# One pool per z operand, mid buffers and first weight units of the way down over early operands, and two pairs made side by side

## The chip, the cores and the metric

The kernel runs on one core of one Trainium2 chip. The metric is the device time of one execution in microseconds (us): the median of three runs is 2313.62 us (2311.71 to 2314.23). The profiled execution, from which all times below come, took 2311.51 us; its span from first to last instruction is 2309.7 us, so 1.8 us lie around the span. Its TensorE clock was 0.983 of full speed in the mean.

## The reference, cut to what matters

One layer of a hybrid decoder for 2048 prompt rows and 8 decode rows, model width 1024, feed-forward width 2816, all float32. Two head groups (windowed attention and gated linear attention) give a mixed activation; what follows is:

```python
def finish(x, o_attn, o_gla, r_gla, gla_norm_g, w_o, ffn_norm_g, w_gate, w_up, w_down):
    g = rmsnorm(o_gla, gla_norm_g).reshape(N, T, GLA_WIDTH) * jax.nn.silu(r_gla)
    h = x + jnp.concatenate([o_attn, g], axis=-1) @ w_o
    z = rmsnorm(h, ffn_norm_g)
    return h + (jax.nn.silu(z @ w_gate) * (z @ w_up)) @ w_down
```

The kernel also returns window buffers and recurrent states; the change does not touch what makes them.

## The kernel before, in words

**Precision and products.** Every float32 operand is split into a high part (a ScalarE cast, L92) and a low part (a VectorE subtraction, L93). A product is three matmuls (`mm3`, L104 to L106). Gate, up and down go by a Strassen–Winograd scheme with seven products P1, P6, P2, P7, P5, P4, P3 in this order (`PRODS`); the class `Strassen` reads each product out of PSUM with additions on VectorE (L961) and, for P1, a copy on ScalarE (L1149). Each product thus has its own operand made from sums of quarter blocks, numbered 0 to 6.

**The stages that matter here.**
1. The W_o stage works row tile by row tile: W_o product (`ps_wo`, the 8 decode rows at L1019), the sum h, RMS normalisation to z, transposes on TensorE (`ps_zT`, L1037). For every group of four tiles `operands()` makes the seven operands, splits each into `zhl` (pool of three buffers) and stores it from GpSimd's DMA queue to DRAM as `zc_d` (L1057). h itself is stored by SyncE (SP) to `h_d` and `hdec_d` (L1022).
2. Gate and up. Per half `sb` of the rows, seven operands z0 to z6 (about 2 MB each) are loaded by SP (L1242) and stay in SBUF. For each of 11 pairs of feed-forward blocks, weights are loaded (`wrg`, L1179), their sums are made and split to `whl`, and `prod` runs 12 matmuls a product. In the first half, gate and up take turns product by product on all 512 columns. In the second half the 516 columns (8 decode rows ride along, four in each block) are two pieces of 258, with all seven products of gate ahead of the seven of up. The result silu(gate)*up is called m; its Strassen sums go from GpSimd's DMA queue to `md_d` (L1236). In the second half the decode columns of m are copied to `mdec` on ScalarE (L1227), four copies of 128x4 a pair, 44 in all.
3. The way down. The 11 pairs are four groups (3, 3, 3, 2 pairs). Per group, weights `wrd` (L1270) become seven units `dhl` a pair, in a pool of 22 buffers; then for each of eight row blocks a 1.3 MB mid `mr` is loaded by SP (L1310), split to seven `dm`, and each product sums its three pairs (9 matmuls). Results are added in DRAM by accumulating DMAs (L1329), and the last group writes the output (L1324). The decode rows' products (L1286) use `mhl`, the split `mdec`.

**What sets the order.** The tile framework records the program and a list scheduler with a model of times writes each engine's instruction list; every engine then works strictly in its list's order. Buffers of stages that have ended are reused by address: a new tile waits for the last reader or writer of whatever lay in its bytes. So the place of a pool in SBUF decides what its first loads wait for. In the kernel before, one pool holds z6 to z0; the pool of weight units comes first in the same space and lies with its first unit over the operand of P4 and then over the operands from P1 on; the two `mr` buffers lie at the other end, over the operands of P4 and P3, which are read last.

## Time and profile before

| | before |
|---|---|
| median of three runs | 2313.62 us |
| profiled execution / its span | 2311.51 / 2309.7 us |
| PE (TensorE matmul) busy | 2227.1 us, 96% |
| DVE (VectorE) busy | 1600.5 us, 69% |
| ACT (ScalarE) busy | 957.2 us, 41% |
| POOL (GpSimd) busy | 623.8 us, 27% |
| gate and up | about 959 to 1847 us |
| way down | about 1853 to 2309 us |

A row of the timeline gives the start, the duration, engine, line, operation, output<-inputs, shape and count; in brackets is the engine's idle time before it and what ended it. A row of the windows view gives the stretch, its length, and then for PE, PEld (weight loads), DVE, ACT and POOL the busy us with the count of instructions, then the granted TensorE clock, the share of the DMA engines' time in use, and GB/s. A row of the waits view gives engine, output, line, what it waited for, and the total, the number and the longest of those waits.

### The profile page before, as it was taken

How to read it: one execution, taken by the hardware profiler on the slowest of the kernel's cores; microseconds unless marked ns; L12 is line 12 of the kernel's file. 1: busy time of each engine (PE TensorE's matmuls, PEld its weight loads, DVE VectorE, ACT ScalarE, POOL GpSimd, SP SyncE). 2: the span in 40 equal slices, each digit the busy share in tenths (PEclk: the TensorE clock that was granted, in tenths of full speed). 3: DMA queues.
4: the chain of work that ended last, by engine and by line, in shares of the span. 5: the costliest groups of instructions: out<-in, count | busy, mean ns of one | idle time of the engine just before them, and what ended most of it. 6: DMA issues, size and time to landing. Idle time of an engine off the chain costs nothing.

```text
span 2309.7 us, 34809 instructions
## 1 busy us (share of the span) xinstructions
PE 2227.1 (96%) x12649; PEld 1923.6 (83%) x12649; DVE 1600.5 (69%) x3236; ACT 957.2 (41%) x2120; POOL 623.8 (27%) x791
## 2 busy tenths in 40 slices
PE   8999998999999999699999999999999989999998
PEld 6888886788887788578888889999999968787887
DVE  6787887587776567556666666767676674847477
ACT  5676777343443234323232333333333243535342
POOL 2443434365465133201111110101010122222222
PEclk9999998999998999899999999999999999999999
DMA  7323234245325689872324257323233277878877
GB/s 239 122 75 115 93 108 153 90 157 165 126 87 214 225 275 288 276 247 87 119 79 127 78 177 290 110 84 115 87 111 97 83 225 171 210 165 213 185 184 263
DMA packets 204935, 364.57 MB, mean 158 GB/s; under 512 B 15411, under 2 KB 128332, under 8 KB 200780
## 3 DMA queue, kind: packets, MB, share of 16 engines
q1 hardware_dynamic: 167740, 258.80, 34.2%
q0 software_dynamic: 37024, 103.55, 17.9%
q8 instruction: 100, 1.64, 0.3%
q14 instruction: 71, 0.58, 0.1%
HBM read 211.09 MB, written 152.27 MB: 157 GB/s over the span
## 4 chain that ended last, share of the span: by engine, by line
PE 31%; issue 20%; POOL 5%; DMA 1%; DVE 0%; POOLq 0%; ACT 0%; SPq 0%; DVEq 0%; ACTq 0%
PE ps_b L105 4%; PE ps_b L104 4%; PE ps_b L106 4%; POOL h_d L1329 4%; PE ps_c L105 3%; PE ps_c L104 3%; PE ps_c L106 3%; PE ps_a L105 3%; PE ps_a L106 3%; PE ps_a L104 3%; POOL out_y_prompt_dram L1324 1%; DMA z<-zc_d_P 1%; POOL md_d L1236 1%; DMA zc_d_P<-zhl 0%; DMA wrg<-in_w_gate_dram 0%
## 5 line engine op out<-in xcount | busy, mean ns | idle before, releaser
L104 PE MATMUL ps_b<-z,whl 128*128 128x258 f32 (+1 forms) x792 | 253.8, 321 | 3.2 <-DMA z<-zc_d_P 3.2
L105 PE MATMUL ps_b<-z,whl 128*128 128x258 f32 (+1 forms) x792 | 254.0, 321 | 0.0
L106 PE MATMUL ps_b<-z,whl 128*128 128x258 f32 (+1 forms) x792 | 252.8, 319 | 0.0
L92 ACT CAST dm<-mr 128x384 fp32r<-128x384 f32 (+1 forms) x224 | 108.0, 488 | 188.4 <-PE ps_b L106 97.6
L104 PE MATMUL ps_a<-z,whl 128*128 128x258 f32 (+1 forms) x528 | 170.9, 324 | 8.3 <-DMA z<-zc_d_P 8.3
L105 PE MATMUL ps_a<-z,whl 128*128 128x258 f32 (+1 forms) x528 | 170.7, 323 | 0.0
L106 PE MATMUL ps_a<-z,whl 128*128 128x258 f32 (+1 forms) x528 | 170.3, 323 | 0.0
L104 PE MATMUL ps_c<-z,whl 128*128 128x258 f32 (+1 forms) x528 | 168.6, 319 | 0.9 <-DMA z<-zc_d_P 0.9
L105 PE MATMUL ps_c<-z,whl 128*128 128x258 f32 (+1 forms) x528 | 169.1, 320 | 0.0
L106 PE MATMUL ps_c<-z,whl 128*128 128x258 f32 (+1 forms) x528 | 168.9, 320 | 0.0
L104 PEld LDWEIGHTS ps_b<-z,whl 128*128 128x128 f32 x792 | 149.3, 189 | 15.9 <-DMA z<-zc_d_P 3.5
L106 PEld LDWEIGHTS ps_b<-z,whl 128*128 128x128 f32 x792 | 149.2, 188 | 12.1
L105 PEld LDWEIGHTS ps_b<-z,whl 128*128 128x128 f32 x792 | 149.2, 188 | 11.9
L93 DVE TENSOR_TENSOR dm<-mr,dm 128x384 fp32r<-128x384 f32 (+1 forms) x224 | 114.9, 519 | 59.4 <-ACT dm L92 59.4
L92 ACT CAST whl<-wrg 128x512 fp32r<-128x512 f32 x132 | 81.6, 620 | 150.5 <-PE ps_b L106 81.2
L802 POOL TENSOR_TENSOR bd<-E,qTb 64x128 f32<-64x128 f32 x224 | 127.1, 567 | 60.6 <-ACT E L787 47.2
L93 DVE TENSOR_TENSOR whl<-wrg,whl 128x512 fp32r<-128x512 f32 x132 | 90.9, 688 | 42.9 <-ACT whl L92 42.7
L961 DVE TENSOR_TENSOR gu<-ps_c,gu 128x512 f32<-128x512 f32 (+1 forms) x130 | 77.9, 600 | 61.0 <-PE ps_c L106 60.3
L1236 POOL DMA_DIRECT2D md_d<-m x22 | 15.7, 713 | 373.7 <-DVE m L1199 360.3
L104 PEld LDWEIGHTS ps_a<-z,whl 128*128 128x128 f32 x528 | 100.8, 191 | 17.0 <-issue 4.4
L104 PEld LDWEIGHTS ps_c<-z,whl 128*128 128x128 f32 x528 | 99.8, 189 | 9.3 <-ACT whl L92 1.3
L105 PEld LDWEIGHTS ps_a<-z,whl 128*128 128x128 f32 x528 | 100.5, 190 | 8.2
(385 smaller groups left out, 6625.9 us busy)
## 6 DMA issues: line engine op xcount, KB each, us to landing
mr<-md_d SPq DMA_DIRECT2D x24, 1344.0 KB
zc_d_P<-zhl POOLq DMA_DIRECT2D x49, 512.0 KB, 6.1
wrg<-in_w_gate_dram SPq DMA_DIRECT2D x44, 512.0 KB
wrg<-in_w_up_dram SPq DMA_DIRECT2D x44, 512.0 KB
nT_d<-nT SPq DMA_DIRECT2D x16, 1024.0 KB
zT<-nT_d SPq DMA_DIRECT2D x8, 2048.0 KB
z<-zc_d_P SPq DMA_DIRECT2D x7, 2064.0 KB
z<-zc_d_P SPq DMA_DIRECT2D x7, 2048.0 KB
```

The lines of the kernel that those rows point to most:

```text
L92: nc.scalar.copy(h, src)
L93: (eng or nc.vector).tensor_tensor(l, src, h.bitcast(F32), ALU.subtract)
L104: nc.tensor.matmul(ps, lh, rh, start=start, stop=False, skip_group_check=more)
L105: nc.tensor.matmul(ps, lh, rl, start=False, stop=False, skip_group_check=more)
L106: nc.tensor.matmul(ps, ll, rh, start=False, stop=stop, skip_group_check=more)
L802: nc.gpsimd.tensor_tensor(bv[rows, :, h], eo, qo, ALU.mult)
L961: nc.vector.tensor_tensor(out, a, b, ALU.add)
L1236: nc.gpsimd.dma_start(md_d[sb][g][:, :, q, fp - GROUPS[g][0], :], src.rearrange("p (m t) -> p m t", m=4))
L1324: nc.gpsimd.dma_start(O["y_prompt"][0, ti * P:(ti + 1) * P, cols], hq[which])
L1329: nc.gpsimd.dma_start(h_d[ti][:, cols], c, accum_op=ALU.add)
```

## The change

1. Each z operand gets a pool of its own, and the pools stand in the order of the products. The addresses of z0 to z6 come out the same.
2. The 44 copies to `mdec` go from ScalarE to GpSimd.
3. On the way down the `mr` pool is placed first, so its two buffers lie over z0 and z1 (read by P1 and P6). The weight units come in three pools of 7, 7 and 8, used in turn; the first unit lies over z2 and z3, the others of the first pair over z1 and z2, the next two pairs over z3 to z6.
4. In the first group the units of pairs 1 and 2 are made side by side, one product of each at a time.

```diff
@@ gate and up
-        zcp = pool(ph, "g_zc", 1, side="right")
+        zcp = {name: pool(ph, f"g_z{q}", 1, side="right") for q, name in enumerate(PRODS)}
...
-                    nc.scalar.copy(mdec[:, 2 * fp + f, 4 * j:4 * j + 4], m[:, 512:516])
+                    nc.gpsimd.tensor_copy(mdec[:, 2 * fp + f, 4 * j:4 * j + 4], m[:, 512:516])
...
-            zc = {name: zcp.tile([P, 2, 4, 516], F32R, tag=f"z{q}", name=f"z{q}")[:, :, :, :WIDTHS[sb]]
-                  for q, name in reversed(list(enumerate(PRODS)))}
+            zc = {name: zcp[name].tile([P, 2, 4, 516], F32R, tag=f"z{q}", name=f"z{q}")[:, :, :, :WIDTHS[sb]]
+                  for q, name in enumerate(PRODS)}
@@ way down
-        wdp = pool(ph, "d_w", 22, side="right")
         mrp = pool(ph, "d_mr", 2, side="right")
+        wdps = [pool(ph, f"d_w{i}", n, side="right") for i, n in enumerate((7, 7, 8))]
+        made = [0]
+
+        def unit_tile():
+            j = made[0] % 22
+            made[0] += 1
+            return wdps[min(j // 7, 2)].tile([P, 2, 512], F32R, tag="w", name="dhl")
...
-            us = []
-            for p in range(p0, p1):
+            us = [{} for p in range(p0, p1)]
+
+            def pair_units(p):
...
-                    hl = wdp.tile([P, 2, 512], F32R, tag="w", name="dhl")
+                    hl = unit_tile()
                     split(hl[:, 0], hl[:, 1], src)
-                    uq[q] = hl
-                us.append(uq)
+                    us[p - p0][q] = hl
+                    yield
+
+            for some in ([[p0], [p0 + 1, p0 + 2]] if g == 0 else [[p] for p in range(p0, p1)]):
+                for _ in zip(*[pair_units(p) for p in some]):
+                    pass
```

The instruction lists differ in two places: where gate and up begin, and where the way down begins (with small moves behind it on the way down). Between them TensorE's list is the same. Line numbers of the changed kernel are 1 higher from L1165 on and 10 to 13 higher on the way down.

**SP where gate and up begin.** `h_d_4838` is the store of the last row tile's h, `hdec_d` that of the decode rows; the numbers 4840 to 4846 at `zc_d_P` are the operands of P1, P6, P2, P7, P5, P4, P3. Before:

```order
L1179 DMA wrg<-in_w_gate_dram 128x4x256
L1022 DMA h_d_4838<-h 128x1024
L1022 DMA hdec_d<-h 8x1024
L1242 DMA z_10184<-zc_d_P_4840 128x8x512
L1242 DMA z_10183<-zc_d_P_4841 128x8x512
L1242 DMA z_10182<-zc_d_P_4842 128x8x512
L1242 DMA z_10181<-zc_d_P_4843 128x8x512
L1242 DMA z_10180<-zc_d_P_4844 128x8x512
L1242 DMA z_10179<-zc_d_P_4845 128x8x512
L1242 DMA z_10178<-zc_d_P_4846 128x8x512
```

And now, in the same place of SP's list:

```order
L1180 DMA wrg<-in_w_gate_dram 128x4x256
L1243 DMA z_10196<-zc_d_P_4840 128x8x512
L1022 DMA h_d_4838<-h 128x1024
L1243 DMA z_10197<-zc_d_P_4841 128x8x512
L1243 DMA z_10198<-zc_d_P_4842 128x8x512
L1243 DMA z_10199<-zc_d_P_4843 128x8x512
L1022 DMA hdec_d<-h 8x1024
L1180 DMA wrg<-in_w_gate_dram 128x4x256
L1180 DMA wrg<-in_w_up_dram 128x4x256
L1243 DMA z_10202<-zc_d_P_4846 128x8x512
L1243 DMA z_10200<-zc_d_P_4844 128x8x512
L1243 DMA z_10201<-zc_d_P_4845 128x8x512
```

The load for P1 moved ahead of the last row tile's store, those for P6, P2 and P7 ahead of the decode rows' store; two weight loads and the load for P3 now stand ahead of those for P5 and P4.

**ACT in the same place.** `zhl` are the casts of the second half's last group of row tiles, `b_9842` to `b_9845` the transposed quarter blocks, `t_10118` to `t_10121` their sums; `gp` is the copy of gate's first product and `whl` are casts of weights. Before:

```order
L1030 ACTIVATE z,ss<-h 8x1024
L92 CAST zhl<-b_9842 128x528
L92 CAST zhl<-t_10119 128x528
L92 CAST zhl<-b_9843 128x528
L92 CAST zhl<-t_10120 128x528
L92 CAST zhl<-t_10118 128x528
L92 CAST zhl<-t_10121 128x528
L92 CAST zhl<-b_9845 128x528
L1149 COPY gp_10193<-ps_a 128x512
```

And now:

```order
L1030 ACTIVATE z,ss<-h 8x1024
L92 CAST whl<-sx 128x512 x2
L92 CAST zhl<-b_9842 128x528
L92 CAST zhl<-t_10119 128x528
L92 CAST zhl<-b_9843 128x528
L92 CAST whl<-sx 128x512
L92 CAST whl<-wrg 128x512
L92 CAST zhl<-t_10120 128x528
L92 CAST zhl<-t_10118 128x528
L92 CAST zhl<-t_10121 128x528
L92 CAST zhl<-b_9845 128x528
L1149 COPY gp_10211<-ps_a 128x512
```

Four casts of weights, whose buffers the products P1 and P6 of gate and up must first release, now stand between and ahead of the `zhl` casts. On TensorE, all 24 matmuls of P1 (and no longer only those of the W_o stage) stand ahead of the decode rows' transposes of z.

**DVE where the way down begins.** `uu`, `gu` and `up` are partial results of up and the products with gate, `dm` the split mids, `dhl` the split weight units, `ty` and `tx` sums of weights. Before, from behind the last product of up on:

```order
L93 TENSOR_TENSOR dhl<-wrd,dhl 128x512
L961 TENSOR_TENSOR up_17944<-gu_17942,gu_17943 128x512
L958 TENSOR_TENSOR uu_17946<-m_17940,gu_17942 128x512
L93 TENSOR_TENSOR dhl<-ty,dhl 128x512
L93 TENSOR_TENSOR dhl<-wrd,dhl 128x512
L958 TENSOR_TENSOR uu_17945<-up_17944,m_17940 128x512
L93 TENSOR_TENSOR dhl<-tx,dhl 128x512
L93 TENSOR_TENSOR mhl<-mdec,mhl 128x22x8
L958 TENSOR_TENSOR ty<-wrd,ty 128x512
L958 TENSOR_TENSOR gu_17942<-gp_17941,uu_17945 128x512
L958 TENSOR_TENSOR tx<-wrd 128x512
L93 TENSOR_TENSOR dm<-mr,dm 128x384 x7
```

And now, from the fourth product of up (P7) on:

```order
L961 TENSOR_TENSOR uu_17964<-ps_b,up_17962 128x258 x2
L93 TENSOR_TENSOR dm<-mr,dm 128x384 x3
L961 TENSOR_TENSOR uu_17964<-ps_c,uu_17964 128x258
L93 TENSOR_TENSOR dhl<-wrd,dhl 128x512
L93 TENSOR_TENSOR dhl<-ty,dhl 128x512
L1200 TENSOR_TENSOR gu_17961<-uu_17964,gu_17961 128x258
L93 TENSOR_TENSOR dhl<-wrd,dhl 128x512
L961 TENSOR_TENSOR uu_17964<-ps_c,uu_17964 128x258
L93 TENSOR_TENSOR dhl<-tx,dhl 128x512
L958 TENSOR_TENSOR ty<-wrd,ty 128x512
L93 TENSOR_TENSOR dm<-mr,dm 128x384
L961 TENSOR_TENSOR up_17962<-ps_b,up_17962 128x258
```

The splits of mids and of the first units moved from behind the last result of up to between the results of its products P7 to P3.

More of the change, by code (lines that the diff above doesn't have):

```diff
@@ L1272, in group @@
                 r0, r1 = raws
-                uq = {}
-                b = (r0[:, 0:512], r0[:, 512:], r1[:, 0:512], r1[:, 512:])
-                for q, src in zip(PRODS, sums_b(*b)):
-                    hl = wdp.tile([P, 2, 512], F32R, tag="w", name="dhl")
+                for q, src in zip(PRODS, sums_b(r0[:, 0:512], r0[:, 512:], r1[:, 0:512], r1[:, 512:])):
+                    hl = unit_tile()
                     split(hl[:, 0], hl[:, 1], src)
-                    uq[q] = hl
-                us.append(uq)
+                    us[p - p0][q] = hl
[3 more added lines that the diff above has]
+                    pass
             def decode():
```

## The prediction

> **What bounds the kernel now.** I read the page first, for the busy shares, then the view of TensorE's waits, then windows over the two places where the instruction lists differ, and then each engine's timeline there.
>
> ```profile
> PE 2227.1 (96%) x12649; PEld 1923.6 (83%) x12649; DVE 1600.5 (69%) x3236; ACT 957.2 (41%) x2120; POOL 623.8 (27%) x791
> ...
> PE ps_a L104 <- DMA z<-zc_d_P: 8.3, 2, 4.3
> ...
> PE ps_zT L1037 <- DVE z L1032: 6.9, 1, 6.9
> PE ps_a L104 <- ACT dm L92: 6.5, 1, 6.5
> ...
> PE ps_b L104 <- DMA z<-zc_d_P: 3.2, 2, 3.0
> ...
> PE ps_c L104 <- ACT dhl L92: 2.2, 1, 2.2
> ...
> PE ps_c L104 <- DMA z<-zc_d_P: 0.9, 1, 0.9
> ```
>
> TensorE is busy 96% of the span, and the change neither adds a matmul nor removes one. Only its idle time and its slow clock can give anything. Four of its waits belong to the start of gate and up (8.3 + 6.9 + 3.2 + 0.9 = 19.3 us, three of them for a z operand), and 6.5 + 2.2 us to the start of the way down.
>
> ```profile
> 940.00:1010.00 70.00, 50.62 (x198) 37.73 (x196) 28.28 (x47) 18.61 (x31) 11.11 (x14) 0.85 0.99 335
> 1820.00:1875.00 55.00, 45.28 (x285) 37.43 (x284) 38.67 (x73) 22.61 (x50) 6.43 (x9) 0.91 0.45 166
> 1875.00:2309.00 434.00, 427.05 (x1879) 346.74 (x1877) 287.11 (x512) 163.90 (x332) 105.30 (x136) 1.00 0.80 198
> ```
>
> In the first window the DMA engines are full (0.99); in the second they are not (0.45). Behind 1875 TensorE is busy 427 of 434 us, so the small moves there can neither win nor lose much; I cost them at 0. That is the cover: if it were gone, the 7 us of idle time in that row would be at stake.
>
> **Part 1, the z operands (about 938 to 1012 us).**
>
> ```profile
> 938.39 7.67 PE L1019 MATMUL ps_wo<-WO,mixdec 128*40 128x512 f32 x32
> ...
> 959.10 0.80 PE L104 MATMUL ps_a<-z,whl 128*128 128x512 f32 x1 [4.28 <-DMA z<-zc_d_P]
> ...
> 970.62 0.51 PE L104 MATMUL ps_b<-z,whl 128*128 128x512 f32 x1 [3.02 <-DMA z<-zc_d_P]
> ...
> 982.03 0.76 PE L104 MATMUL ps_a<-z,whl 128*128 128x512 f32 x1 [4.03 <-DMA z<-zc_d_P]
> ...
> 996.34 0.47 PE L104 MATMUL ps_c<-z,whl 128*128 128x512 f32 x1 [0.93 <-DMA z<-zc_d_P]
> ...
> 938.52 0.33 SPq L1022 DMA_DIRECT2D h_d<-h  x1
> 950.34 0.29 SPq L1022 DMA_DIRECT2D hdec_d<-h  x1
> 950.81 40.70 SPq L1242 DMA_DIRECT2D z<-zc_d_P  x7
> ```
>
> P1 begins at 959.10, P6 at 970.62, P2 at 982.03, P5 at 996.34; each needs about 5.5 us of TensorE (24 matmuls at 0.23 us), so 959 to 982 holds 11 us of work. The first load leaves SP only behind the decode rows' store, at 950.81, and P1 starts 8.3 us later. In the changed list that load stands ahead of the last tile's store (938.52) and waits only for the W_o matmuls whose weights lie in its bytes, so it can leave near 938 and land by 950.
>
> P1 then waits for something else, a PSUM bank that VectorE frees with the first low-part addition of the decode rows:
>
> ```profile
> 947.61 0.68 DVE L582 TENSOR_TENSOR h<-ps_wo,h 8x512 f32<-8x512 f32 x1
> ...
> 954.69 0.63 ACT L92 CAST zhl<-b 128x528 fp32r<-128x528 f32 x1 [3.20 <-issue]
> ...
> 964.68 0.63 ACT L92 CAST zhl<-t 128x528 fp32r<-128x528 f32 x1 [6.61 <-DMA zc_d_P<-zhl]
> ...
> 974.71 0.63 ACT L92 CAST zhl<-b 128x528 fp32r<-128x528 f32 x1 [3.45 <-DMA zc_d_P<-zhl]
> 975.25 0.58 ACT L1149 COPY gp<-ps_a 128x512 f32<-128x512 f32 x1
> ```
>
> That is 948.3, so P1 runs from about 949 to 955, ten us earlier than before, and P6 when z1 lands (issued behind the decode matmuls at 946, so by about 957). This gain does not reach the end of the stage. P2 reuses the bank that ScalarE's copy of P1 frees, and this copy stands in ScalarE's list behind the last `zhl` cast (974.71 here), which waits for a `zhl` buffer and so for an earlier store to `zc_d` to land. Before, that was hidden, since z2 came at 982.03. In the changed order it becomes the gate, and it slips: two weight casts that wait for P1, and two that wait for P6, now stand among the `zhl` casts, and on TensorE the decode rows' transposes, from which all of these casts come, stand behind P1. By hand, P1's end at 955 to 956.5 against the first `zhl` cast's 954.69 shifts the chain by 1.5 to 3.5 us, the copy ends at 977.3 to 979.3, and P2 starts near 978: **4 us** earlier than 982.03. P5, at 996.34 before, follows two products later at about 992. Its load waits for its own store, the third from the end, and by my replay lands by 990, so it doesn't decide. On SP it now stands behind the load for P3 and behind two weight loads, which wait for buffers that VectorE frees once P6 is done, near 964; neither is due before 990 either. Bounds: if P2 starts no earlier than before, 0; if the chain doesn't slip (P2 at 975.9) and TensorE stays at full clock, 6 us, and 8 if the 0.93 us before P5 and the slow stretch behind P2's pause go as well.
>
> The clock is part of that price.
>
> ```profile
> 960.00:965.00 5.00, 5.00 (x13) 3.84 (x13) 0.00 (x0) 0.32 (x1) 0.71 (x1) 0.51 1.03 373
> ...
> 980.00:985.00 5.00, 2.97 (x7) 2.42 (x8) 0.80 (x2) 0.00 (x0) 0.00 (x0) 0.70 1.06 327
> ```
>
> Behind P1's pause 13 matmuls took 5 us at clock 0.51 where 0.23 us each makes 3.0; behind P2's, 7 took 2.97 us where 1.6 would do. A pause of about 4 us is thus followed by a slow stretch that costs 1.3 to 2 us and more. In the changed kernel P2 follows one pause of some 14 us; I charge it the stretch that it had before (1.3); were it twice as long, 1.3 us of the 4 would go, which the bounds hold. By the Trainium skill, "TensorE: Matmul & The Clock Gate" (Part 1, the HAM clock gate), the clock drops to half after an idle window of about 3.4 us and comes back after as long a busy one, whatever the length of the pause; by that one long pause costs no more than a short one, about 1.7 us, and the sum would change by less than half a us. The row of 960 to 965 agrees in kind, though at half clock for all of its 5 us.
>
> **Part 2, the copies to mdec.**
>
> ```profile
> 1836.01 0.19 ACT L1227 COPY mdec<-m 128x4 f32<-128x4 f32 x1 [5.84 <-DVE m L1199]
> ...
> L802 POOL TENSOR_TENSOR bd<-E,qTb 64x128 f32<-64x128 f32 x224 | 127.1, 567 | 60.6 <-ACT E L787 47.2
> ...
> L1236 POOL DMA_DIRECT2D md_d<-m x22 | 15.7, 713 | 373.7 <-DVE m L1199 360.3
> ```
>
> 44 copies of 0.19 us are 8.4 us off ScalarE, which is 41% busy: no gain in themselves. On GpSimd the trace has no such copy; the nearest row is a 64x128 operation of 0.57 us, 32 times as wide, so each costs something between nothing and 0.6 us. It sits idle for 360 us before the `md_d` stores, so 0 either way. What the move does is clear ScalarE's list: the copy shown waited 5.84 us for a result, and everything behind it with it. Through that they belong to part 3.
>
> **Part 3, the start of the way down.**
>
> ```profile
> 1847.05 0.80 SPq L1310 DMA_DIRECT2D mr<-md_d  x2
> ...
> 1852.95 2.99 ACT L92 CAST dm<-mr 128x384 fp32r<-128x384 f32 x7 [4.36 <-DMA mr<-md_d]
> ...
> 1853.52 0.80 PE L104 MATMUL ps_a<-dhl,dm 128*128 128x512 f32 x1 [6.50 <-ACT dm L92]
> ...
> 1847.06 0.43 DVE L961 TENSOR_TENSOR uu<-ps_c,uu 128x258 f32<-128x258 f32 x1 [0.55 <-PE ps_c L106]
> ...
> 1854.13 3.36 DVE L93 TENSOR_TENSOR dm<-mr,dm 128x384 fp32r<-128x384 f32 x7
> ```
>
> Before, the first `mr` leaves at 1847.05, when the last z operand is read, and lands 5.9 us later (1852.95); TensorE stands from 1847.0 to 1853.52.
>
> ```profile
> 1835.00:1840.00 5.00, 5.00 (x44) 5.00 (x43) 1.42 (x4) 0.19 (x1) 0.71 (x1) 1.00 0.18 52
> ...
> 1850.00:1855.00 5.00, 1.48 (x4) 0.90 (x5) 5.00 (x10) 2.05 (x5) 2.32 (x4) 0.50 0.99 390
> 1855.00:1860.00 5.00, 5.00 (x14) 3.07 (x13) 5.00 (x11) 4.59 (x10) 0.00 (x0) 0.58 1.03 401
> 1860.00:1865.00 5.00, 2.77 (x12) 1.41 (x10) 4.32 (x8) 2.05 (x4) 0.00 (x0) 1.00 0.99 382
> ...
> 1870.00:1875.00 5.00, 4.68 (x19) 2.81 (x19) 4.94 (x9) 2.74 (x6) 0.59 (x1) 1.00 0.00 0
> ```
>
> From 1850 to 1860 VectorE is full, and up to 1875 TensorE runs 12 to 19 matmuls in 5 us where it could run 22: the stage is bound by the splits. About 67 matmuls are done from 1847 to 1875; at 0.23 us they are 15.4 of 28 us, so 12.6 us are lost.
>
> In the changed kernel the `mr` buffers lie over z0 and z1, free when up's P6 has been read. Up's products take 2.9 us each (24 matmuls at 0.12 us) and the last ends at 1847.0, so P6, five products ahead, ends at about 1833; the load lands 5.9 us later, at 1839, with the DMA engines at 0.18. Seven `dm` splits (3.36 us on VectorE) and four units (4 x 0.6 us) then run before 1847, in a VectorE that is busy 1.42 of 5 us: 5.8 us of the work that bound the stage moves ahead. The first product can start once VectorE has read the last of P3 (1847.06 before, about 1.5 us later with the splits between), near 1849 against 1853.52. Replaying the list from there I count 57 matmuls by 1865 and a full TensorE behind, against 67 by 1875; 57 x 0.23 is 13.1 of 18, so 4.9 us are lost in place of 12.6. That is 7.7 us; I take **7**, as the second part of VectorE's list is rough. Bounds: 3 us, if only the earlier start of 4.5 counts and the units of pairs 1 and 2 give some back, and 10, if all waits and the slow clock go and only the start at 1849 is left. Side-by-side units are in this count: each product needs the units of three pairs.
>
> **The sum.** 4 + 7 = 11 us, from the profiled 2311.51 to 2300.5. The median of the runs lies 2.1 us above the profiled run, which would make it 2302.6. I say **2302 us**.
>
> **The rivals.** (a) The forecast, 2302, with 2298 to 2306 as its own range.
>
> (b) Only the way down gains. P2 starts at 982 as before, because the `zhl` stores, which share full DMA engines with loads that now start 13 us earlier, land later. For it: the DMA engines are at 0.99 in that window. Against: before 955 the trace has room. Time: 2313.6 - 7 = 2306.6.
>
> (c) Both gain at their bound: 8 + 10 = 18, so 2295.6. Against it, the chain of `zhl` casts can hardly fail to slip.
>
> (d) The change doesn't do what it says: the way down stays bound by VectorE (3 us gained) and the z operands give 0: 2310.6. VectorE's row of 1870 to 1875, still 4.94 of 5 us busy, speaks for it.
>
> (e) Slower, by one mechanism: the slow `zc_d` store.
>
> ```profile
> zc_d_P<-zhl POOLq DMA_DIRECT2D x7, 528.0 KB, 9.4
> zc_d_P<-zhl POOLq DMA_DIRECT2D x6, 512.0 KB, 5.2
> ```
>
> Stores to `zc_d` land in 5.2 us in the median without z loads beside them and in 9.4 us with them. Two landings in a row stand between the third and the last `zhl` cast, and the last cast gates P2. From 978 each further us of landing delays P2 by two: at 2 us more the first part gains nothing, and only from about 8 us more (17 us each) is P2 12 us later than before, which outweighs the 7: 2313.6 - 7 + 12 = 2318.6. By the Trainium skill, "DMA: Bandwidth & Descriptors" (Queues, rings and completion order), an engine takes turns between the queues that have work, packet by packet. By that a store beside one queue of loads gets half the rate however many loads stand behind, so its landing should stay near 9.4 us, which speaks against (e); the two rows above agree, no run yet shows it with earlier loads.
>
> **How the numbers follow.** (a) 0.57, (b) 0.20, (c) 0.08, (d) 0.09, (e) 0.06. About 0.2%, 4.6 us, is what a measurement of this kernel can tell from no change. Faster by more than that: (a), (b) but for its upper edge, and (c), 0.83. Within it: (d) and that edge, 0.13. Slower: most of (e), 0.04. Case (a) and most of (b) and (c) make the range 2295 to 2309.
>
> **What would show it.** In the changed profile: the first z load near 938 and P1 near 949; TensorE's longest wait there before P2, near 978, ended by ScalarE's `gp` copy and not by a z load; P5 at about 992. On the way down: `mr` issued near 1833 less the 4 us of the first part, the `dm` casts about 6 us behind, the first matmul within 2.5 us of the last of up, no slow clock there, and TensorE full from 18 us behind the last of up. Wrong would be: a TensorE pause before up's P3 (mids that land more than 3 us late would hold VectorE ahead of the additions that free its banks), `zc_d` landings above 12 us, or a window on the way down behind 1875 with less than the 427 of 434 us.

## The result, and the profile after

The changed kernel is slower: a median of 2319.06 us (ten runs, 2314.7 to 2322.57) against 2312.1 us for the kernel before in the same rounds (ten runs, 2309.08 to 2316.36). The ratio is 1.0029 with a 95% interval of 1.0019 to 1.0038, so some 7 us were lost where 11 were forecast as gained. The profiled execution has a span of 2317.4 us, 7.7 us more than before.

The page of the changed kernel (first row) and its view of TensorE's waits:

```profile
PE 2221.5 (96%) x12649; PEld 1916.7 (83%) x12649; DVE 1595.7 (69%) x3236; ACT 951.2 (41%) x2076; POOL 642.7 (28%) x835
...
PE ps_a L104 <- ACT gp L1149: 23.1, 2, 22.9
...
PE ps_b L104 <- DMA z<-zc_d_P: 1.7, 1, 1.7
...
PE ps_a L104 <- DMA z<-zc_d_P: 1.1, 1, 1.1
```

TensorE's busy time is about what it was (2227.1 us before). The waits for a z operand (8.3 + 3.2 + 0.9 us over five places before) have shrunk to 1.7 + 1.1 us, and the 6.5 us for `dm` are gone. In their place stands one wait of 22.9 us for ScalarE's copy `gp`, the largest of the whole program. The windows view shows in which stretch the time went; the kernel before first, then the changed one:

```profile
935.00:1010.00 75.00, 55.62 (x224) 41.49 (x223) 31.71 (x53) 18.69 (x31) 13.67 (x17) 0.86 0.96 323
```

```profile
935.00:1010.00 75.00, 44.29 (x181) 32.64 (x181) 30.45 (x50) 18.68 (x31) 12.65 (x16) 0.77 0.98 320
...
1875.00:2318.00 443.00, 431.51 (x1889) 347.89 (x1887) 290.47 (x519) 166.01 (x337) 105.88 (x136) 1.00 0.78 195
```

Where gate and up begin, 181 matmuls were done in 75 us where 224 had been; at 0.23 us each the 43 missing ones are 9.9 us. Behind 1875 TensorE is now idle for 443 − 431.5 = 11.5 us instead of 7.

To compare runs I use stretches between events, since the part up to the W_o stage, whose instruction lists are the same in all kernels here, scatters by −4.2 to +3.6 us from one profiled execution to another. The first stretch goes from the last W_o matmul of a row tile to the last matmul of up: 909.64 us before (937.38 to 1847.02), 919.48 us after (935.05 to 1854.53), **+9.8 us**. From there on I follow ScalarE's copy `c<-ps_a`, of which there is one a row block, eight a group. The rows of the eighth, sixteenth and twenty-fourth, before and after:

```profile
1973.62 0.59 ACT L1327 COPY c<-ps_a 128x512 f32<-128x512 f32 x1
...
2094.39 0.59 ACT L1327 COPY c<-ps_a 128x512 f32<-128x512 f32 x1
...
2214.64 0.59 ACT L1327 COPY c<-ps_a 128x512 f32<-128x512 f32 x1
```

```profile
1976.63 0.59 ACT L1340 COPY c<-ps_a 128x512 f32<-128x512 f32 x1
...
2097.40 0.59 ACT L1340 COPY c<-ps_a 128x512 f32<-128x512 f32 x1
...
2219.72 0.59 ACT L1340 COPY c<-ps_a 128x512 f32<-128x512 f32 x1 [0.59 <-PE ps_a L106]
```

From the end of up to the eighth copy it is 126.60 us before and 122.10 after: **−4.5 us**, the gain at the start of the way down. The next group costs the same in both, the third 122.32 against 120.25 us (**+2.1**), and the stretch to the last store of the output another **+2.6 us**. Together +10.0 us, of which the early scatter of this profile (937.38 to 935.05, −2.3) leaves the 7.7 us between the spans.

**Where the 22.9 us come from.** First TensorE at the start of gate and up, in the changed kernel's timeline, then SP's issues there:

```profile
935.05 0.39 PE L106 MATMUL ps_wo<-WO,mt 128*128 128x512 f32 x1
...
951.81 0.77 PE L104 MATMUL ps_a<-z,whl 128*128 128x512 f32 x1 [1.08 <-DMA z<-zc_d_P]
...
991.05 0.80 PE L104 MATMUL ps_a<-z,whl 128*128 128x512 f32 x1 [22.89 <-ACT gp L1149]
```

```profile
935.47 0.59 SPq L1243 DMA_DIRECT2D z<-zc_d_P  x1
...
943.77 14.81 SPq L1243 DMA_DIRECT2D z<-zc_d_P  x3
958.68 4.64 SPq L1022 DMA_DIRECT2D hdec_d<-h  x1
963.42 0.76 SPq L1180 DMA_DIRECT2D wrg<-in_w_gate_dram  x1
...
978.66 19.63 SPq L1243 DMA_DIRECT2D z<-zc_d_P  x3
```

The loads do leave early (935.47 against 950.81), and P1 starts at 951.81 against 959.10. P2 waits for the bank that `gp` reads. ScalarE and VectorE, the changed kernel:

```profile
960.69 0.63 ACT L92 CAST zhl<-b 128x528 fp32r<-128x528 f32 x1
...
989.88 0.63 ACT L92 CAST zhl<-b 128x528 fp32r<-128x528 f32 x1 [11.54 <-DMA zc_d_P<-zhl]
990.42 0.58 ACT L1149 COPY gp<-ps_a 128x512 f32<-128x512 f32 x1
...
980.62 0.69 DVE L958 TENSOR_TENSOR sy<-wrg,sx 128x512 f32<-128x512 f32 x1 [11.08 <-DMA wrg<-in_w_gate_dram]
...
982.23 2.59 POOL L1057 DMA_DIRECT2D zc_d_P<-zhl  x3 [14.74 <-DVE zhl L93]
```

Read backwards: `gp` stands behind the last `zhl` cast; that cast waits until an earlier `zhl` buffer has been stored; the store waits for VectorE's `zhl` subtractions; and VectorE had been idle for 11.08 us, because a sum of the *second* pair's weights stands ahead of three of them in its list and the load of those weights, issued at 963.42 behind the three z loads and the `hdec_d` store, landed only at 980.6, 17 us later. On top of that the chain starts late: the first `zhl` cast is at 960.69 instead of 954.69.

### The profile page after: what moved, and what is told of

Its sections match the earlier page's. It is cut to its first block, busy times and chain, and to the rows that moved or that the text cites. A ratio compares the mean times of both kernels' runs of the same rounds, so it can differ in the third digit from the quotient of the medians.

```text
span 2317.4 us, 34789 instructions
## 1 busy us (share of the span) xinstructions
PE 2221.5 (96%) x12649; PEld 1916.7 (83%) x12649; DVE 1595.7 (69%) x3236; ACT 951.2 (41%) x2076; POOL 642.7 (28%) x835
## 4 chain that ended last, share of the span: by engine, by line
PE 77%; issue 6%; DVE 6%; DMA 5%; POOL 3%; ACT 2%; SPq 0%; POOLq 0%; DVEq 0%; ACTq 0%
PE ps_b L105 7%; PE ps_b L104 7%; PE ps_b L106 7%; PE ps_a L105 5%; PE ps_a L104 5%; PE ps_a L106 5%; PE ps_c L105 5%; PE ps_c L104 5%; PE ps_c L106 5%; PE ps_d L104 3%; PE ps_d L106 3%; PE ps_d L105 3%; PE ps_wo L104 2%; PE ps_wo L106 2%; PE ps_wo L105 2%
## 5 line engine op out<-in xcount | busy, mean ns | idle before, releaser
L104 PE MATMUL ps_a<-z,whl 128*128 128x258 f32 (+1 forms) x528 | 170.7, 323 | 24.0 <-ACT gp L1149 22.9
L104 PEld LDWEIGHTS ps_a<-z,whl 128*128 128x128 f32 x528 | 100.8, 191 | 33.1 <-ACT gp L1149 23.3
L92 ACT CAST whl<-sy 128x512 fp32r<-128x512 f32 x88 | 54.7, 621 | 152.3 <-PE ps_b L106 88.7
L105 PEld LDWEIGHTS ps_a<-z,whl 128*128 128x128 f32 x528 | 100.4, 190 | 8.2
L106 PEld LDWEIGHTS ps_a<-z,whl 128*128 128x128 f32 x528 | 100.3, 190 | 7.8
```

Of the source, the lines that this page charges most:

```text
L92: nc.scalar.copy(h, src)
L104: nc.tensor.matmul(ps, lh, rh, start=start, stop=False, skip_group_check=more)
L105: nc.tensor.matmul(ps, lh, rl, start=False, stop=False, skip_group_check=more)
L106: nc.tensor.matmul(ps, ll, rh, start=False, stop=stop, skip_group_check=more)
```

## The experiments

Each kernel was timed in five rounds beside the kernel before; ratios are to it, with their 95% interval. `issue_after(x)` in the diffs puts an instruction behind x in the list of the same engine and adds nothing else. One table of stretches for all of them, each as the difference to the kernel before, from the profiled executions:

| kernel | W_o to end of up | to end of group 1 | group 2 | group 3 | to the end | ratio |
|---|---|---|---|---|---|---|
| the change | +9.8 | −4.5 | 0.0 | +2.1 | +2.6 | 1.0029 |
| e1 | +8.2 | −2.6 | 0.0 | 0.0 | +0.1 | 1.0026 |
| e2 | −0.4 | −3.6 | +0.8 | +2.4 | +1.5 | 0.9997 |
| e3 | +4.7 | −6.0 | −0.6 | +1.9 | +2.0 | 1.0015 |
| e4 | +0.6 | −2.5 | +3.8 | +2.0 | +2.7 | 1.0019 |
| e5 | +0.3 | −3.6 | +2.9 | +2.1 | +0.9 | 0.9997 |
| e6 | −0.6 | −3.3 | +0.9 | +3.6 | +1.0 | 1.0007 |
| e7 | +7.0 | −6.0 | −0.4 | +1.8 | +1.5 | 1.0007 |
| e8 | −0.2 | −3.6 | +1.6 | 0.0 | 0.0 | 0.9993 |
| e9 | +0.1 | 0.0 | −0.1 | 0.0 | 0.0 | 1.0001 |
| e11 | +8.0 | −4.3 | −0.7 | 0.0 | 0.0 | 1.0012 |
| e12 | +7.3 | −3.6 | −0.7 | 0.0 | +1.2 | 1.0017 |
| e13 | −0.4 | −3.2 | +0.2 | +0.5 | 0.0 | 0.9975 |
| e14 | −2.5 | −3.7 | −0.7 | +0.6 | +0.1 | 0.9964 |
| e15 | −3.9 | −8.2 | +0.5 | +2.0 | +1.3 | 0.9970 |

The sum of a row lies within 1.5 us of the difference of the medians for ten of the fifteen, and 1.9 to 3.3 us off for the change, e5, e7, e13 and e14; so single entries under about 2 us are not read as effects. e2 and e5 show why: they differ only in the engine of the `mdec` copies and have the same ratio, and yet stand 2.1 us apart in group 2.

### e1: the z pools alone

```diff
 kernel before, with
-        zcp = pool(ph, "g_zc", 1, side="right")
+        zcp = {name: pool(ph, f"g_z{q}", 1, side="right") for q, name in enumerate(PRODS)}
```

> The kernel before with the first part of the change alone (a pool for each z operand); the copies to mdec, the mr pool, the unit pools and the order of the units stay as before. Where gate and up begin, the instruction lists of SP, ACT, DVE and PE come out as in the changed kernel. Theory: the loss is made at this place. The load of the second pair's weights stands on SP behind three z loads; VectorE's list has the sum of these weights ahead of three low parts of zhl; so the stores to zc_d, the last zhl cast, the gp copy and P2 are late. Then P2 starts near 991 as in the changed kernel (982.0 before), and the time is 7 to 9 us above the kernel before, about 2320. Rival: the loss is made on the way down, and this kernel is within 2 us of the kernel before or faster by up to 4.

Measured: 2316.57 against 2310.72 us, ratio 1.0026 (1.0016 to 1.0036). TensorE in its timeline:

```profile
989.59 0.79 PE L104 MATMUL ps_a<-z,whl 128*128 128x512 f32 x1 [22.07 <-ACT gp L1149]
```

The same picture as in the changed kernel, with 8.2 of its 9.8 us; VectorE stands 10.10 us for the second pair's weights. One part of the change, the z pools, carries the loss, some 6 us here where 7 to 9 were expected.

### e2: everything but the z pools

```diff
 the change, with
-        zcp = {name: pool(ph, f"g_z{q}", 1, side="right") for q, name in enumerate(PRODS)}
+        zcp = pool(ph, "g_zc", 1, side="right")
```

> The changed kernel without its first part: one pool for the seven z operands as before, but the copies to mdec on GpSimd, the mr buffers over z0 and z1, unit pools and units of pairs 1 and 2 side by side. Theory: the start of the way down gains about 4 us (the lag of the changed kernel falls from 7.5 us at the last products of up to 3.5 us at the end of the first group), and up to 4 us of it are lost again where later groups begin; so 0 to 4 us below the kernel before. Rival, the prediction's count for this part: 7 us below. Rival on the other side: this part is what makes the changed kernel slow, 3 us or more above the kernel before.

Measured: 2309.91 against 2310.72 us, 0.9997 (0.9989 to 1.0006), no difference. The start of gate and up is as before (−0.4 us). The start of the way down gains 3.6 us, and groups 2 to 4 give 4.7 back (0.8 + 2.4 + 1.5). One thing limits this run as a trial of the rest. The mids do load 14.4 us ahead of the end of up, but the splits of mids and units stand behind it in VectorE's list: VectorE is busy for 5.10 of the last ten us of up, as in the kernel before, and for 8.99 in the change. e4, e5, e6, e8 and e9 share this order, so none of them has the list that the prediction replayed. Two questions were left: what at the start of gate and up makes the early loads harmful, and what the later groups lose on.

### e3: the second pair's weight work behind the last zhl subtraction on VectorE

```diff
 the change, with
+                if (sb, fp) == (0, 1):
+                    with tc.issue_after(last_zhl_subtraction):
+                        pair(sb, fp, zc)
```

> The changed kernel with one edge more: VectorE's work on the second pair of gate and up stands behind the last low part of zhl in VectorE's list, so that no zhl waits for the load of these weights. SP's and ACT's lists stay. Theory (VectorE held by the weight sum): the idle time of 11.1 us ahead of three zhl parts goes, P2 starts near 979 to 982 in place of 991, and the time falls by 8 to 10 us against the changed kernel, to about 2310. Rival (the stores to zc_d land late because the z loads fill the DMA engines, as the prediction's slower case has it): the stores take as long to land, P2 starts within 2 us of 991 and the time stays at 2317 to 2319.

Measured: 2313.5 against 2310.72 us, 1.0015 (1.0005 to 1.0025). In its timeline P2 still waits, but less:

```profile
986.53 0.80 PE L104 MATMUL ps_a<-z,whl 128*128 128x512 f32 x1 [16.38 <-ACT gp L1150]
```

Counted from the last W_o matmul (937.89 here) P2 comes at 48.6 us, against 56.0 in the changed kernel and 44.7 before. The sum that waits for the late weight load is thus worth 7.4 of the 11.4 us at P2 and 5.1 us of the stretch (9.8 to 4.7), where 8 to 10 us had been expected. It is the largest single piece, but not all; and since the stores still land beside early loads here, slower stores aren't the main cause.

### e7: all of that weight work behind the last zhl, on ScalarE too

```diff
 e3, and
+                if 7 <= made_u[0] < 28:   # units 8 to 28: the rest of the first pair's, the second's
+                    behind the last zhl cast (ScalarE) and subtraction (VectorE)
```

> The whole change, with all weight work of the first pair from its eighth unit on and of the second pair behind the last zhl on both ScalarE and VectorE, so that the zhl chain waits for neither P1, P6 nor a weight load; on SP one weight load in place of two stands ahead of the last z loads. Theory: the chain starts some 6 us earlier than in the run where only VectorE's work was moved, P2 starts near 979, the stretch from the last W_o tile to the last product of up takes 908 to 911 us (919.5 in the changed kernel, 914.3 with only VectorE's work moved, 909.6 before), and the time is 2 us above to 3 us below the kernel before. Rival (the DMA engines bound this stage, so the loads land no earlier and P2 only moves to about 984): 2 to 4 us above.

Measured: 2315.34 against 2313.36 us, 1.0007 (0.9997 to 1.0017).

```profile
981.92 0.80 PE L104 MATMUL ps_a<-z,whl 128*128 128x512 f32 x1 [13.04 <-ACT gp L1157]
...
977.20 0.52 SPq L1251 DMA_DIRECT2D z<-zc_d_P  x1
982.23 0.39 SPq L1188 DMA_DIRECT2D wrg<-in_w_gate_dram  x1
988.06 5.22 SPq L1251 DMA_DIRECT2D z<-zc_d_P  x2
```

P2 is at 44.9 us behind the last W_o matmul, as early as before; the slipped casts were another 3.7 us. Yet the stretch still costs +7.0 us, more than in e3, where 2 us less to 1 us more than before had been expected. The reason is the second piece of the same mistake: P5, two products on, waits 5.1 us for its operand, whose load stands on SP behind the load for P3 and a weight load. It leaves 51.1 us behind the last W_o matmul, against 42.5 in the kernel before.

### e11: the decode rows' transposes ahead of P1, and one unit pool

```diff
 e7, with one pool of 22 units on the way down as before, and
+                if (sb, fp) == (0, 0):
+                    with tc.issue_after(last_transpose):
+                        pair(sb, fp, zc)
```

> The whole change with one pool for the units, the zhl chain ahead of later weight work on ScalarE and VectorE, and on TensorE the decode rows' transposes ahead of P1, so that the chain of zhl waits for nothing that comes from the early loads. z loads stay early. Theory A (the early loads are worth what room the DMA engines had, 2.8 us by their shares between 940 and 955, and only what stood ahead of the zhl chain spoiled it): P2 starts near 978, the stretch from the last W_o tile to the last product of up takes 906 to 909 us (909.6 before), the way down gains 6 us and keeps them; 6 to 9 us below the kernel before. Theory B (earlier loads slow the stores to zc_d and h_d and give nothing): the stretch takes 910 us or more; 4 to 6 us below.

Measured: 2313.8 against 2311.13 us, 1.0012 (1.0003 to 1.002).

```profile
978.40 0.79 PE L104 MATMUL ps_a<-z,whl 128*128 128x512 f32 x1 [7.71 <-ACT gp L1158]
...
1001.52 0.76 PE L104 MATMUL ps_c<-z,whl 128*128 128x512 f32 x1 [9.57 <-DMA z<-zc_d_P]
```

The `zhl` chain is repaired: P2 comes at 41.3 us, 3.3 us earlier than before, which is what the prediction had expected of it (978). All of it is lost again at P5, which waits 9.57 us, and the stretch still stands at +8.0. Two gates lie side by side at this place; opening this one alone does not bring the stretch back. No run opens the other one alone.

### e12: the z loads behind the decode rows' store

```diff
 e11, and
+                if sb == 0:
+                    with tc.issue_after(hdec_d_store):
+                        the seven z loads
```

> The run with the transposes first, with the one difference that all seven z loads stand behind the store of the decode rows' h on SP, as in the kernel before. Theory A: the stretch from the last W_o tile to the last product of up takes 909 to 911 us as before, 2 to 3 us more than with the early loads; the way down gains 6 us; 5 to 6 us below the kernel before. Theory B: no slower than with the early loads.

Measured: 2314.6 against 2311.13 us, 1.0017 (1.0008 to 1.0026). The early loads are gone and the loss is not (+7.3 us, where theory A had none); P5 waits again:

```profile
998.69 0.77 PE L104 MATMUL ps_c<-z,whl 128*128 128x512 f32 x1 [6.48 <-DMA z<-zc_d_P]
```

So what is left of the loss does not need loads that leave early, nor the DMA time that these take from others; the candidate that remains is the order of the last three z loads among themselves and against the weight loads.

### e13: z loads in the products' order, the second pair's weights behind them, all behind the store

```diff
 e12, and
+                each z load behind the one of the product before; the second pair's wrg loads behind the last
```

> The run with the z loads behind the decode rows' store, with one difference: on SP the seven z loads go in the order of the products and the second pair's weight loads stand behind all of them, as in the kernel before (there the load for P3 and a weight load stood ahead of those for P5 and P4, and P5 waited 6.5 us for its operand). Theory: the stretch from the last W_o tile to the last product of up is 909 to 911 us as in the kernel before (917.0 with the load for P3 ahead); the way down gains 3 to 5 us and keeps them, since it has one pool of units; 3 to 5 us below the kernel before. Rival: the stretch stays above 912 us, and the place of the load for P3 was not its cause.

Measured: 2308.37 against 2314.32 us, 0.9975 (0.9966 to 0.9985). Nothing waits for P5's operand any more, and the stretch is back at −0.4 us. The edit from e12 to e13 touches SP's order alone: it is worth 7.7 us. The load for P5 now leaves 42.1 us behind the last W_o matmul, where it left at 48.0 in e12. The edit moves the load for P3 and the weight loads at once, so the two are not told apart.

### e14: the same with the early loads

```diff
 e13 without "behind the store": the first four z loads leave as early as in the change
```

> As the run with the z loads in turn, but the first four of them early as the change has them: ahead of the last tile's and the decode rows' stores. The one difference between the two is when the loads can leave. Theory A (early loads win the room that the DMA engines had): the stretch is 906 to 908.5 us, 2 to 3 us less than with the late loads, and the time 5 to 8 us below the kernel before. Theory B (the stage is bound by the DMA engines and the chain of stores, early loads win nothing): within 1 us of the run with late loads.

Measured: 2304.86 against 2314.32 us, 0.9964 (0.9951 to 0.9977). Its timeline:

```profile
978.72 0.80 PE L104 MATMUL ps_a<-z,whl 128*128 128x512 f32 x1 [8.78 <-ACT gp L1158]
...
944.96 14.15 SPq L1256 DMA_DIRECT2D z<-zc_d_P  x3
...
979.38 9.19 SPq L1256 DMA_DIRECT2D z<-zc_d_P  x3
988.63 8.00 SPq L1189 DMA_DIRECT2D wrg<-in_w_gate_dram  x2
```

SP is held for 14.15 us by three loads just as in the changed kernel, but what stands behind them is no longer needed soon. P2 is at 978.7, and the stretch gains 2.5 us. With the late loads of e13 it was −0.4, so the early loads win some 2 us, about as much as single entries can show; the medians of the same rounds, 2304.86 and 2308.37, go the same way, though their intervals overlap.

### e4, e5, e6: the parts of the way down, and the loads of later groups

```diff
 e4: e2, with every pair's units made one pair after the other
 e5: e2, with nc.scalar.copy(mdec...) as before
 e6: e2, and in groups 2 and 3
+                if g in (1, 2) and mi == 1: the second mid's load behind the fifth weight load of the group
```

> The kernel before with the copies to mdec on GpSimd, the mr buffers over z0 and z1 and the unit pools, but the pairs' units one after the other; z operands in one pool as before. Against the run without the z pools (which had the pairs side by side and was 0.8 us below the kernel before, with 4 us gained at the start of the way down and given back where the third and fourth groups begin). Theory: side by side costs. Pair 2's weights cannot be loaded until pair 0 has given back two of the four raw buffers (VectorE stood 3.9 us for that load), and SP's list of the third group puts two mids ahead of weight loads; without it SP's list of the third group is again as in the kernel before. So 3 to 6 us below the kernel before. Rival: side by side is what gives the 4 us, and without it the time is within 1 us of the kernel before.

> The kernel before with the mr buffers over z0 and z1, the unit pools and the pairs side by side, but the copies to mdec on ScalarE as before; z operands in one pool. Theory: the copies matter only through ScalarE's list at the start of the way down, where casts of mids and units would wait behind copies of up's results; 1 to 3 us slower than with the copies on GpSimd, so 0 to 2 us above the kernel before. Rival: the copies matter nowhere, and it is within 0.7 us of the run with the copies on GpSimd (2309.9 there, 0.8 below the kernel before).

> The change without its z pools, and with one thing more: in the second and third groups the second mid's load stands on SP behind the weight load that stands ahead of it in the kernel before as well. Theory: the 4 us gained at the start of the way down are given back because two mids' loads, of which the second waits for its buffer, hold up the weight loads of the third group; with the old order about 2.5 us of them stay, so 2 to 4 us below the kernel before. Rival: they are lost to something else (VectorE has too much to do where groups meet), and the time stays within 0.7 us of 2309.9.

Measured, against 2313.36 us: e4 2319.53, 1.0019 (1.001 to 1.0029); e5 2313.41, 0.9997 (0.9988 to 1.0006); e6 2314.53, 1.0007 (0.9998 to 1.0016). Without the units side by side (e4) the kernel is slower than e2's 0.9997; neither the theory nor the rival had that. The profile has 3.0 us of it in group 2, but e5, with side by side, has 2.9 there as well, so the place is open. The copies to `mdec` change nothing that can be told on either engine (0.9997 in e2 and e5, each within 0.0009). In e6 group 3 loses 3.6 us where e2 loses 2.4: the weight loads that stand behind a mid on SP are not what the later groups lose on, a miss of mine.

### e8, e9: one pool of units instead of three

```diff
 e2, with
-        wdps = [pool(ph, f"d_w{i}", n, side="right") for i, n in enumerate((7, 7, 8))]
+        wdp = pool(ph, "d_w", 22, side="right")
+        spare = wdp.tile(...)      # first buffer set aside, it lies over the operand read last
 e9: e8, with the units one pair after the other
```

> The change without its z pools, and with the weight units of the way down in one pool of 22 buffers again (a buffer that is touched once first keeps the place over z6 out of the first units' way, so the first units still lie over z0 to z4). In the three pools of the change a unit of a later group takes the buffer of the unit 22 places back, so that the units of pair 0 wait for pair 0's products one by one and pair 1 for the last product of the group; the one pool gives each unit the buffer that came free first. Theory: this throttling is where the 4 us gained at the start of the way down go (0.8, 2.4 and 1.5 us at the three later groups). With one pool the lag stays as it is from the end of the first group on, and the time is 3 to 5 us below the kernel before. Rival: where groups meet, VectorE and the weight loads cannot keep up whatever the buffers; then the time stays within 1.5 us of the kernel before.

> The same with one pool, but the units of pairs 1 and 2 of the first group one after the other. Theory: with one pool the later groups lose nothing here either; what is left is what side by side is worth at the start, 1 us (2.5 against 3.6 us gained by the end of the first group in the runs with three pools); so 2 to 4 us below the kernel before. Rival (the 6 us between the two runs with three pools came from side by side itself): 1 us below to 3 us above the kernel before.

Measured, against 2311.13 us: e8 2308.64, 0.9993 (0.9984 to 1.0001); e9 2310.95, 1.0001 (0.9992 to 1.001). e8's interval reaches from 3.7 us below the kernel before to 0.2 above, so the 3 to 5 us expected are not shown; e9 comes out as its rival had it. In e9 the twenty-fourth `c` copy comes 367.6 us behind the end of up, as in the kernel before (2214.64 − 1847.02), and e8 too loses nothing in groups 3 and 4, where e2 loses 3.9 us and the change 4.7. That loss belongs to the three pools. In group 2 the entries (+0.8 in e2, +1.6 in e8) are too small to tell. How it comes about, the programs tell. In the kernel before, a unit gets the buffer that came free first, and the products free one buffer of each of the three pairs in turn, so group 2's units follow the products across the pairs. With three pools used in turn, unit number j always gets the buffer of unit j − 22: the first pair's units wait for the first pair's products one by one, to the end of the old group. In the changed kernel ScalarE's casts of units wait for a product twice, 4.0 us in all, behind 1875 (first row below; 4.0 to 4.9 us in e2, e3 and e15, no such row in the kernel before, e8 and e14). TensorE waits five times there, 4.0 us in all (0.9 us before), 2.1 us of it for units:

```profile
ACT dhl L92 <- PE ps_b L106: 4.0, 2, 2.0
...
PE ps_b L104 <- DVE gu L961: 1.9, 2, 1.0
...
PE ps_b L105 <- DVE dhl L93: 1.0, 1, 1.0
...
PE ps_c L104 <- ACT dhl L92: 0.6, 1, 0.6
...
PE ps_a L105 <- DVE dhl L93: 0.5, 1, 0.5
```

e9 against e8 prices the units side by side, with one pool: 0.0 against −3.6 us at the start of the way down, so the early mids alone (e9) are worth nothing there. With three pools e4 gains 2.5 us without side by side and e2 3.6 with it, so this price holds for one pool only.

### e15: e14 with the change's three unit pools

```diff
 e14, with the three pools of 7, 7 and 8 units
```

> The run with early z loads in turn, with one difference: the three unit pools of the change in place of the one. Theory: the three pools alone cost what the later groups lose; the lag at the end of the first group is as with one pool or up to 1 us better, then 0.5 to 1 us are lost at the second group, about 2 at the third and about 1.5 at the fourth; 4 to 5 us below the kernel before in place of 8. Rival: the later losses of the changed kernel hung on its other lists, and this run is within 1 us of the one with one pool.

Measured: 2303.53 against 2310.66 us, 0.9970 (0.996 to 0.9979). The later groups lose about what was expected, but the start of the way down gains 4.5 us more than in e14, where up to 1 was expected. The changed kernel's rows around the end of up (1854.53), and then e15's (1840.10):

```profile
1844.53:1854.53 10.00, 10.00 (x84) 9.79 (x82) 8.99 (x20) 5.30 (x11) 0.00 (x0) 1.00 0.46 184
1854.53:1864.53 10.00, 7.58 (x29) 4.70 (x30) 10.00 (x21) 4.66 (x10) 7.82 (x9) 1.00 0.81 250
1864.53:1869.53 5.00, 2.30 (x11) 1.56 (x9) 1.03 (x3) 0.53 (x2) 0.87 (x2) 1.00 0.77 295
...
1870.00:1875.00 5.00, 4.24 (x10) 2.46 (x11) 4.96 (x9) 3.63 (x8) 0.00 (x0) 0.69 0.34 105
```

```profile
1840.10:1850.10 10.00, 7.50 (x29) 4.62 (x30) 9.94 (x21) 4.59 (x10) 7.76 (x9) 1.00 0.78 266
1850.10:1860.10 10.00, 7.97 (x33) 5.28 (x32) 7.99 (x14) 5.09 (x10) 0.97 (x2) 1.00 0.51 186
```

For ten us behind the end of up (second row above, first row below) the two are the same. Then VectorE in the changed kernel runs dry (1.03 of 5 us busy), for the load of the third pair's weights; its row in the changed kernel and the one in e15:

```profile
1868.69 0.69 DVE L958 TENSOR_TENSOR tx<-wrd 128x512 f32<-128x512 f32 x1 [3.94 <-DMA wrd<-in_w_down_dram]
```

```profile
1852.35 0.69 DVE L958 TENSOR_TENSOR tx<-wrd 128x512 f32<-128x512 f32 x1 [1.91 <-DMA wrd<-in_w_down_dram]
```

Behind the end of up that is 14.2 us against 12.3: 1.9 us later. TensorE pauses for it and runs slowly afterwards (0.69 of its clock in the last row above, ten matmuls in 4.24 us where 2.3 would do, 1.9 us more). In e3 and e7, whose lists on VectorE, ScalarE, GpSimd and SP are the change's from the start of the way down to the end of the third group, the same sum comes 12.7 and 12.5 us behind the end of up (1852.18 in e3), and both gain 6.0 us:

```profile
1864.93 0.69 DVE L958 TENSOR_TENSOR tx<-wrd 128x512 f32<-128x512 f32 x1 [2.35 <-DMA wrd<-in_w_down_dram]
```

So the later landing is worth about 1.5 of the 3.7 us between −4.5 and −8.2, and among kernels with these lists it is seen in the one profiled execution of the changed kernel alone. The pair's two loads are issued 0.5 and 5.2 us behind the end of up in the changed kernel, 0.6 and 5.3 in e15; why they land at different times no run here tells. The other 2.2 us go with a different order: from 15.5 us behind the end of up on, e15's VectorE list takes some splits of mids before splits of units, where the change takes the units first. No run tries that order by itself.

The three pools give 4.5 us more than e14's single pool there and 3.8 less in the later groups (+0.5 + 2.0 + 1.3 against 0.0), and e14 and e15 come out alike within their intervals. The gain goes with VectorE's list: in e15 the splits of the first five units stand ahead of the end of up (8.99 of the last ten us busy), in e14 only those of mids (7.57). e2 and e8, which have neither, show no difference between three pools and one (−3.6 both). e14 and e15 both beat the kernel before and the change.

## Why the prediction was wrong, by its steps

**Part 1, the z operands: forecast −4 us, measured +9.8. This is the step that failed.** Its first half came true in kind: the first load left at 935.47, and the wait ahead of P2 was ended by the `gp` copy, not by a z load. But P1 began 16.8 us behind the last W_o matmul, earlier than before (21.7) and later than forecast (949 − 937.4 = 11.6): its load, counted at 12 us, took 16.3, and two of the weight casts ahead of the first `zhl` cast wait for P1. The sentence that failed is the one on SP's list: the two weight loads and the load for P3 that stand ahead of P5's, "neither is due before 990 either". I asked only when TensorE needs them. VectorE needs the second pair's weights much earlier, since its list has that pair's sum ahead of three `zhl` subtractions, and its list is strict; a load that I took for slack was the gate of the chain. It held VectorE for 11.08 us, and putting the sum behind won 5.1 us (e3). The slip of the `zhl` chain, costed at 1.5 to 3.5 us, was 6 us by the first cast (954.69 to 960.69), with a last W_o matmul that came 2.3 us earlier; e7 and e11 together won 7.3 us at P2. And P5's load, the other part of that sentence, was a second gate of 5 to 10 us that lay hidden behind the first in the changed kernel (e7, e11, e12). With both gates open (e14, e15) P2 starts 42.5 and 40.2 us behind the last W_o matmul, where 40.6 was forecast (978 − 937.4), and the stretch gains 2.5 and 3.9 us, where 4 was. So the gain was there; the two orders that the scheduler wrote around it, VectorE's and SP's, cost some 12 to 14 us (9.8 and the 2.5 to 3.9).

What is a little open: P2 behind the last W_o matmul differs by 2.3 us between e14 and e15 (42.5 and 40.2), which differ there in nothing that I changed, so the split between the casts (3.7) and the transposes (3.6) is rough.

**The clock's price: right.** One pause of 22.9 us was followed by no more slow time than the pauses of 4 us before. The changed kernel behind P2's start at 991.05:

```profile
990.00:995.00 5.00, 3.95 (x10) 3.13 (x11) 1.91 (x3) 2.77 (x4) 0.85 (x1) 0.53 0.74 188
```

Ten matmuls in 3.95 us instead of 2.3 are 1.65 us (in the next 5 us the clock was 1.00). The rule of the Trainium skill, "TensorE: Matmul & The Clock Gate" (Part 1, the HAM clock gate), by which a busy window brings the clock back however long the pause was, agrees with that number in kind. The size varies: in the runs here 7 to 14 slow matmuls (3.0 to 6.1 us) follow a pause, 14 of them behind the 22.07 us in e1 and behind the 5.1 us ahead of P5 in e7.

**Part 2, the copies to mdec: right as far as it was tried.** 0 either way, within 2 us (e5 against e2). Both have the old order on VectorE at the end of up, so the copies were not tried in the changed kernel's own order.

**Part 3, the start of the way down: right in kind, mis-sized in the change.** Forecast −7 (7.7 counted, bounds 3 to 10), measured −4.5. Its first steps came as told. `mr`, the `dm` casts and the first product in the changed kernel:

```profile
1840.17 0.80 SPq L1323 DMA_DIRECT2D mr<-md_d  x2
...
1845.78 1.35 ACT L92 CAST dm<-mr 128x384 fp32r<-128x384 f32 x3 [8.10 <-DMA mr<-md_d]
...
1855.94 0.47 PE L104 MATMUL ps_a<-dhl,dm 128*128 128x512 f32 x1 [1.41 <-DVE uu L961]
```

The load leaves 14.4 us ahead of the end of up (14 forecast), lands 5.6 us later (5.9), and the first product starts 1.4 us behind the last of up (2 to 2.5). What was too large is the VectorE work moved ahead: 8.99 us busy in the last ten us of up against 5.10 before, so 3.9 us net where 5.8 were counted. The replay was too fast as well: it had 57 matmuls done 18 us behind the end of up, and the windows view gives 43 in the changed kernel, 47 in e3 and 51 in e15. (The 67 of the kernel before, from 1847 to 1875, were too many too: a single window gives 59.) And no step of mine had the third pair's weights late; that cost VectorE 3.94 us, and TensorE, which then paused for 3.3 us, ran at 0.69 of its clock from 1870 to 1875, against "no slow clock there". With the same lists e3 and e7 have −6.0, so this order gives 4.5 to 6 us where 7 was forecast, inside the bounds; e15's −8.2, near the 7.7 counted, belongs to another order and does not confirm the count. The kernel before, for the comparison of VectorE's 5.10:

```profile
1837.02:1847.02 10.00, 10.00 (x84) 9.79 (x82) 5.10 (x12) 2.12 (x6) 1.42 (x2) 1.00 0.21 69
```

**"Small moves behind 1875" at 0: wrong, +4.7 us.** I named the cover, 427 of 434 us busy, and the 7 us that could be at stake, but looked there for a gain and not for what three pools do when the buffers come round again. The front page named the pools' order of use; the price was never worked out. With one pool the third and fourth group lose nothing (e8, e9), and with three they lose again (e15).

**The rivals.** (e), with a chance of 0.06, had the sign, the place (P2 behind the `gp` copy) and nearly the time (2318.6 against 2319.06), but not the mechanism: it needed stores to `zc_d` that land in 17 us, so the near time is luck. The stores landed in 9.3 us in the median, beside 9.4 before with loads:

```profile
zc_d_P<-zhl POOLq DMA_DIRECT2D x7, 528.0 KB, 9.3
zc_d_P<-zhl POOLq DMA_DIRECT2D x6, 512.0 KB, 9.3
```

The rule of the Trainium skill by which the landing should stay near 9.4 us, "DMA: Bandwidth & Descriptors" (Queues, rings and completion order), agrees with these two rows. The fault of method: having ruled out the store, I gave the whole slower side 0.04, without asking of every instruction that the new order put ahead of the `zhl` chain, on each engine, what it waits for.

## What to carry to other kernels

When a change lets loads leave earlier, list everything that now stands behind them in the issuing queue and ask which engine's *list*, not which product, needs it first: an in-order engine stops at an instruction that nobody needs yet, and what stands behind it is late. Two gates at one place hide each other, so an experiment that opens one and shows nothing has not cleared it (e11, with one gate open, stands at +8.0 us, e14, with both, at −2.5). Splitting a pool of buffers that is used round and round fixes which old buffer each new tile waits for; against a single pool the split cost 2.6 to 3.9 us in the third and fourth group (e15 against e14, e2 against e8).

## What the runs showed of the hardware that was not expected

The issuing itself can hold the engine that issues. In the changed kernel the issues of three 2 MB loads took SP 14.81 us, and the issue of the 32 KB store behind them 4.64 us, where it took 0.29 us before, ahead of the loads. The 512 KB weight load issued next, at 963.42, landed 17 us later. The early load of P1's operand, issued at 935.47, was there at 951.81, 16.3 us later, where the one issued at 950.81 before took 8.3 us; half of the 15 us of lead was lost that way.

Stores of 512 KB to `zc_d` landed in 5.2 us in the median before and in 9.3 us beside the early loads, while those of 528 KB stayed at 9.3 (9.4 before): the price of a store had already reached its level beside the first loads, and earlier loads did not raise it.
